# A streaming encoder layer (RWKV-7 and forgetting attention): modulation tiles in groups, and the steps of each stage given one by one

## The chip, the cores and the metric

The kernel runs on one core of a Trainium2 chip. The metric is the device time of one execution, in microseconds (us). The kernel before takes 1701.49 us, the median of 3 runs (1700.19 to 1702.09); the profiled execution took 1699.15 us.

## The reference, cut to what matters

One layer of width 1024 over 1024 prompt frames of one stream and 64 new frames of another (with 256 past frames in a cache). `c` is a conditioning vector for each stream; the six modulation vectors that come of it are what the change groups.

```
mod = silu(c) @ w_ada + b_ada                       # 1024 -> 6 x 1024, per stream
sh1, sc1, gt1, sh2, sc2, gt2 = split(mod, 6)
h = rms_norm(x, norm1_g) * (1 + sc1) + sh1
proj = h @ w_in                                     # RWKV: r, k, v, three small ones; FoX: q, k, v, f
z = p + (previous row of p - p) * shift_mu          # the RWKV columns
... decay, a, g from small two-layer products; kk = normalized k
y_rwkv = (groupnorm(scan of s = s*w + (s @ -kk)(kk*a) + v k) + bonus) * g      # 8 heads x 64
y_fox = softmax(q k / 8 + decay bias, causal) @ v                              # 8 heads x 64
x = x + gt1 * (concat(y_rwkv, y_fox) @ w_out)
h2 = rms_norm(x, norm2_g) * (1 + sc2) + sh2
x = x + gt2 * ((silu(h2 @ w_gate) * (h2 @ w_up)) @ w_down)
```

Outputs are x and the new states, keys, values and log forget values, all in fp32.

## The kernel before, in words

Activations lie with the 1024 columns on partitions (8 tiles of 128, index k) and the frames along the free axis. Half 0 is the prompt's frames 0 to 511, half 1 the frames 512 to 1023 with the 64 new frames behind them (576, in two pieces of 288). Large products keep fp32 accuracy by splitting both operands into a high and a low part: `mm3` (L289 to L296) issues three matmuls for each k, whi times xhi (L294), whi times xlo (L295), wlo times xhi (L296). `split` casts the high part on ScalarE (L212) and subtracts on VectorE (L216).

**Modulation.** `mod` has 48 column tiles of 128: 0 to 7 are sh1, 8 to 15 sc1, 16 to 23 gt1 and so on. For one tile, `ada_mm` (L182) issues 8 matmuls with 32 columns of `ct` as the stationary operand (columns 0 and 1 are silu(c) of the two streams, the others zero); four k at a time write four strips of 32 partitions. ScalarE copies the result into `mrow` (L193). `ada_fin` (L195) transposes it on TensorE (L198), sums the four strips on VectorE (`mred`, L200) and adds the bias (`mod`, L201). `gains` (L203, L204) makes (1 + sc) * norm_g.

**The stages.**
1. The start: x is loaded and its statistics are taken; the 16 tiles of sh1 and sc1 are computed in the order 0, 8, 1, 9, ...; whenever a pair is there, `h_part` makes that k's part of h: x times gain on VectorE (L270), `hhi` on ScalarE (L271), `hlo` on VectorE (L272). Two w_in tiles (12 and 13) are split beside it.
2. Phase of half 0, then of half 1: `phase` (L1295) walks the string ORDER[half], whose letters are steps for a pair of heads: Z the three RWKV projections, D, A, B, N the decay, the chunk matrices, the scan, the output norm, Q, K, V, q, k the FoX projections and norms. `proj` (L298) takes one modulation tile off a list (`background`, tiles 16 to 39) before each w_in tile that it loads in half 0.
3. Attention of half 0, then of half 1: `Pipe` keeps three units (a pair of query blocks of a head) in flight. After head 0's units of half 1, `residual_x` and `load_mix` bring in half 0's rows: `load_mix` (L980) reads 8 tiles of 128 x 512 from a scratch in HBM (L984) through a pool of two buffers ("fs") and splits each (`mixrh`, `mixrl` for RWKV, `mixfh`, `mixfl` for FoX). Then after every head comes one `outproj` tile of half 0 (`po`).
4. The output projection of half 1, the FFN (tiles 40 to 47 of the modulation, gt2, are computed at its start: 40 to 43 among half 0's first FFN products and 44 to 47 before half 1's), and the down projection.

A tile scheduler sets the order of the instructions on every engine. It works from the order in which the program issues them and from modelled finish times, so a step that is issued earlier is spread among what stands there. Each engine then executes its own list in order, and a transfer is issued from SP's list, in order as well.

Of the kernel before, what the change touches and what calls it, by code (L numbers as in the profile page):

```python
# [16 lines left out]
P = 128  # L17
# [17 lines left out]
ORDER = ("Z0 D0 A0 D1 Z1 L Q0 B0 V0 N0 A1 C0 Z2 D2 q0 O A2 K0 k0 B1 K1 V2 Z3 D3 Q1 q1 V1 C1 A3 S k1 Q2 N1 q2 Q3 B2 N2 K2 k2 V3 K3 k3 C2 q3 C3",  # L35
         "Z0 T3 L D0 A0 Z1 U3 D1 B0 Q0 A1 D2 K0 Z2 A2 k0 D3 Q1 q0 N0 B1 K1 k1 q1 Z3 A3 N1 V0 V1 B2 V2 Q2 N2 q2 K3 Q3 q3 P B3 K2 k3 k2 V3")
# [28 lines left out]
class K:  # L65
# [7 lines left out]
    def consts(self):  # L73
# [14 lines left out]
        self.ct = c.tile([P, KT, 32], F32, name="ct")  # L88
        nc.gpsimd.memset(self.ct, 0.0)
        nc.vector.tensor_tensor(self.ct[:, :, 0:2], cc.rearrange("p (b k) -> p k b", b=2),  # L90
# [90 lines left out]
    def ada_mm(self, t, raw=None, ptag="mm"):  # L181

        nc = self.nc
        if raw is None:
            raw = self.ada_load(t)
        ps = self.ps([P, 2, P], tag=ptag, name="pada")
        for s in range(2):
            for i in range(4):
                k = 2 * i + s
                last = nc.tensor.matmul(ps[32 * i:32 * i + 32, 0], self.ct[:, k], raw[:, k], start=(s == 0),  # L190
                                        stop=(s == 1))
        row = self.slot([P, P], name="mrow", tag="mrow")
        return t, ps, row, last, nc.scalar.copy(row, ps[:, 0])  # L193

    def ada_fin(self, part):  # L195
        nc = self.nc
        t, ps, row = part[:3]
        self.last = nc.tensor.transpose(ps[:, 1], row, self.ident)  # L198
        red = self.slot([P, 2], name="mred", tag="mred")
        nc.vector.tensor_reduce(red, ps[:, 1].rearrange("p (i b) -> p b i", i=4)[:, 0:2], axis=AX.X, op=ALU.add)  # L200
        nc.vector.tensor_scalar(self.mod[:, t], red, self.vc[:, V_BADA + t:V_BADA + t + 1], None, op0=ALU.add)  # L201
# [215 lines left out]
    def rwkv_a(self, hf, j, z, d):  # L417
# [29 lines left out]
        for h in range(2):  # L447
# [6 lines left out]
            bon[:, off:off + m], ps, zv[:, off:off + m], op=ALU.mult), "ra")  # L454

        At = self.rpool.tile([P, 9, 2, 2, 64], F32, tag="At", name="At")
        for c in range(0, nch, 4):
# [7 lines left out]
            for h in range(2):  # L465
                nc.vector.tensor_tensor(At[:, c:c + m, :, h], pa[h][:, 0:m].rearrange("p i (x t) -> p i x t", x=2),
                                        self.amask[:, h:h + 1].rearrange("p o (x t) -> p o x t", x=2)
                                        .to_broadcast([P, m, 2, 64]), op=ALU.mult)

# [30 lines left out]
    def rwkv_b(self, hf, j, st):  # L500
# [14 lines left out]

        def small(name, blocks, mm):
# [20 lines left out]
        for h in range(2):  # L537
            for x in range(2):
                r = 64 * h + 32 * x
                nc.scalar.copy(inv[r:r + 16, 0:nch, r + 16:r + 32], pg[h][r:r + 16, 0:nch, 16:32])  # L540

# [16 lines left out]
        nc.gpsimd.memset(rk[64:128, 0:nch, 0:64], 0.0)  # L558

# [9 lines left out]
        for t0 in range(0, nch, 8):  # L569
# [6 lines left out]
            for x in range(min(2, m)):  # L576
                for h in range(2):
                    nc.scalar.copy(sv[64 - 64 * h:128 - 64 * h, t0 + x:t0 + m:2, h],
                                   pt[64 * x:64 * x + 64, 0:(m - x + 1) // 2, 64 * h:64 * h + 64])

# [8 lines left out]
        for c in range(nch):  # L589
            if c == 8:  # L590
# [385 lines left out]


# [310 lines left out]
    def phase(self, hf, order, late):  # L1288
# [13 lines left out]
        d, z, st, y, y0, f = {}, {}, {}, {}, {}, {}  # L1302
        for t in order:
            op, j = t[0], int(t[1]) if len(t) > 1 else 0
            if op == "D":
                d[j] = self.rwkv_d(hf, j, zl)
            elif op == "Z":
                zk = self.proj_z(hf, 4 + j)
                sq = self.slot(name="sq", tag="sa")
                nc.scalar.activation(sq[:, 0:hf.n], zk[:, 0:hf.n], AF.Square, scale=self.vc[:, V_KK + j:V_KK + j + 1])  # L1310
                z[j] = zk, self.proj_z(hf, j), self.proj_z(hf, 8 + j), sq
            elif op == "A":
                st[j] = self.rwkv_a(hf, j, z.pop(j), d.pop(j))
            elif op == "B":
                y[j] = self.rwkv_b(hf, j, st.pop(j))
            elif op == "N":
                self.rwkv_n(hf, j, y.pop(j), zg)
            elif op == "T":
# [404 lines left out]
```

## Time and profile before

| | |
|---|---|
| median of 3 runs | 1701.49 us |
| profiled execution, its own time | 1699.15 us |
| its span, first to last instruction | 1697.5 us |
| mean granted TensorE clock | 0.992 |
| TensorE matmul busy | 1645.3 us, 97% |
| VectorE, ScalarE, GpSimd busy | 1124.8, 726.5, 183.1 us |

The kernel spends 0 to 36 us in the start, to about 334 in the phase of half 0, to about 737 in that of half 1 (the attention of half 0 lies over its end, from about 665 to 745), to about 905 in the attention of half 1 and half 0's output projection, to 953 in half 1's output projection; the FFN takes it to 1431 and the down projection to the end. A row of the timeline gives the start, the duration, the engine, the line of the code, the operation, output<-inputs and in brackets the idle time of the engine just before, with what ended it. A row of the windows gives busy time and number of instructions of each engine in that stretch, then the granted clock, the share of DMA time and GB/s.

### The profile page before, as it was taken

Reading aid. Unit: us, or ns where it says so; the run is one execution under the profiler, and the core shown is the slowest. Engines: PE = TensorE matmul, PEld = TensorE weight load, DVE = VectorE, ACT = ScalarE, POOL = GpSimd, SP = SyncE. Lnnn points to the kernel's source line nnn. Section 1 sums busy time; section 2 is a strip of 40 time slices with the busy share of each in tenths; the row PEclk is TensorE's granted clock in tenths of the full one; section 3 lists DMA queues with packets and bytes.
Section 4 is the critical chain, followed back from the end, with each engine's and each line's share of the span. In section 5 each row is a group of like instructions: output and inputs, shape, how many; then the busy total and the mean of one; then the engine's idle time right before and its main releaser. Section 6 shows DMA issues by size and latency. Waiting matters only on the chain.

```text
span 1697.5 us, 33265 instructions
## 1 busy us (share of the span) xinstructions
PE 1645.3 (97%) x12897; PEld 1439.1 (85%) x12897; DVE 1124.8 (66%) x2573; ACT 726.5 (43%) x1530; POOL 183.1 (11%) x412
## 2 busy tenths in 40 slices
PE   6999999999999999989999999999999999999999
PEld 3776776788888888767889899999999999999998
DVE  6776676757867655877877975555555556545545
ACT  4535364653545346766776633333333333211210
POOL 2102230222121213201120000000000000000000
PEclk9999999999999999989999999999999999999999
DMA  8544447541233344566654432222222215323313
GB/s 308 164 128 133 141 135 200 176 123 33 71 85 85 87 135 113 149 190 179 169 181 167 157 127 77 77 77 77 77 77 77 77 65 196 134 79 97 97 40 121
DMA packets 133580, 207.08 MB, mean 122 GB/s; under 512 B 62126, under 2 KB 70350, under 8 KB 133422
## 3 DMA queue, kind: packets, MB, share of 16 engines
q1 hardware_dynamic: 133422, 204.95, 39.5%
q8 instruction: 102, 1.67, 0.4%
q14 instruction: 56, 0.46, 0.1%
HBM read 157.65 MB, written 47.25 MB: 121 GB/s over the span
## 4 chain that ended last, share of the span: by engine, by line
PE 84%; DVE 6%; ACT 4%; DMA 3%; issue 2%; SPq 0%; POOL 0%; ACTq 0%; DVEq 0%; POOLq 0%
PE pd L1275 15%; PE pfe L1160 8%; PE pfc L1160 7%; PE pfa L1160 7%; PE pmm L294 5%; PE pmm L295 5%; PE pmm L296 5%; PE pfb L1160 4%; PE pbs L375 2%; PE pav L962 2%; PE po L294 2%; PE ppt L940 2%; PE po L296 2%; PE po L295 2%; PE pA L464 2%
## 5 line engine op out<-in xcount | busy, mean ns | idle before, releaser
L294 PE MATMUL pmm<-hhi,whi 128*128 128x288 f32 (+1 forms) x624 | 218.8, 351 | 2.3 <-ACT pb L317 1.4
L295 PE MATMUL pmm<-hlo,whi 128*128 128x288 f32 (+1 forms) x624 | 217.0, 348 | 0.0
L296 PE MATMUL pmm<-hhi,wlo 128*128 128x288 f32 (+1 forms) x624 | 215.2, 345 | 0.6 <-DVE wlo L216 0.6
L212 ACT CAST whi<-wraw 128x1024 fp32r<-128x1024 f32 (+2 forms) x116 | 99.2, 855 | 212.5 <-PE pd L1275 167.0
L1275 PE MATMUL pd<-ah,wlo 128*128 128x512 f32 (+1 forms) x528 | 173.5, 329 | 0.0
L1275 PE MATMUL pd<-al,whi 128*128 128x512 f32 (+1 forms) x528 | 173.3, 328 | 0.0
L1275 PE MATMUL pd<-ah,whi 128*128 128x512 f32 (+1 forms) x528 | 173.1, 328 | 0.0
L1279 DVE SCALAR_TENSOR_TENSOR x1t<-pd,mod,x1t 128x512 f32<-128x512 f32 x192 | 91.4, 498 | 111.5 <-PE pd L1275 111.0
L294 PEld LDWEIGHTS pmm<-hhi,whi 128*128 128x128 f32 x624 | 119.0, 191 | 14.1 <-ACT pb L317 2.0
L296 PEld LDWEIGHTS pmm<-hhi,wlo 128*128 128x128 f32 x624 | 118.7, 190 | 10.9 <-issue 1.7
L295 PEld LDWEIGHTS pmm<-hlo,whi 128*128 128x128 f32 x624 | 118.7, 190 | 9.9 <-issue 1.2
L216 DVE TENSOR_TENSOR wlo<-wraw,whi 128x1024 fp32r<-128x1024 f32 (+2 forms) x108 | 104.2, 965 | 18.8 <-ACT whi L212 18.3
L1275 PEld LDWEIGHTS pd<-al,whi 128*128 128x128 f32 x528 | 99.4, 188 | 7.7
L1275 PEld LDWEIGHTS pd<-ah,whi 128*128 128x128 f32 x528 | 99.3, 188 | 7.7
L1275 PEld LDWEIGHTS pd<-ah,wlo 128*128 128x128 f32 x528 | 99.3, 188 | 7.5
L1160 PE MATMUL pfc<-hh,hS 128*128 128x256 f32 (+1 forms) x352 | 101.6, 289 | 1.6 <-ACT hh L1062 1.6
L1160 PE MATMUL pfc<-hl,hS 128*128 128x256 f32 (+1 forms) x352 | 101.9, 289 | 0.0
L1160 PE MATMUL pfa<-hh,whi 128*128 128x256 f32 (+1 forms) x352 | 101.9, 290 | 0.0
L1160 PE MATMUL pfa<-hl,whi 128*128 128x256 f32 (+1 forms) x352 | 101.8, 289 | 0.0
L1160 PE MATMUL pfc<-hh,lS 128*128 128x256 f32 (+1 forms) x352 | 101.5, 288 | 0.0
L1160 PE MATMUL pfa<-hh,wlo 128*128 128x256 f32 (+1 forms) x352 | 101.4, 289 | 0.0
L604 POOL TENSOR_SCALAR sd<-sv,pc 64x64 f32<-64x64 f32 x136 | 76.3, 561 | 181.2 <-DVE sv L617 157.6
(361 smaller groups left out, 4383.5 us busy)
## 6 DMA issues: line engine op xcount, KB each, us to landing
wraw<-in_w_in_dram SPq DMA_DIRECT2D x52, 512.0 KB
wada<-in_w_ada_dram SPq DMA_DIRECT2D x48, 512.0 KB
as<-actscr SPq DMA_DIRECT2D x22, 544.0 KB
wraw<-in_w_gate_dram SPq DMA_DIRECT2D x22, 512.0 KB
wraw<-in_w_up_dram SPq DMA_DIRECT2D x22, 512.0 KB
wraw<-in_w_down_dram SPq DMA_DIRECT2D x40, 256.0 KB
wraw<-in_w_out_dram SPq DMA_DIRECT2D x16, 512.0 KB
actscr<-sg SPq DMA_DIRECT2D x22, 288.0 KB
```

The source lines that it names most:

```text
L212: nc.scalar.copy(hi, src)
L216: eng.tensor_tensor(lo, src, hi.bitcast(F32), op=ALU.subtract)
L294: nc.tensor.matmul(ps[0:M, 0:n], whi[:, k, 0:M], xhi[:, k, off:off + n], start=(k == 0), stop=False)
L295: nc.tensor.matmul(ps[0:M, 0:n], whi[:, k, 0:M], xlo[:, k, off:off + n], start=False, stop=False)
L296: nc.tensor.matmul(ps[0:M, 0:n], wlo[:, k, 0:M], xhi[:, k, off:off + n], start=False, stop=(k == kt - 1))
L375: nc.tensor.matmul(ps[:, 0:n], w, x[:, off:off + n], start=True, stop=True)
L464: nc.tensor.matmul(pa[h][:, i], kb[hp, c + i], rk[hp, c + i], start=True, stop=True)
L604: nc.gpsimd.tensor_scalar(sd[hsl[h]], sv[hsl[h], c, h], pc[hsl[h], c], None, op0=ALU.mult)
L940: nc.tensor.transpose(pt[0:rows, b - b0, t * P:t * P + qn], p[0:qn, pc:pc + rows], self.ident[0:qn, 0:qn])
L1160: nc.tensor.matmul(ps, l[:, k], r[:, s, k], start=(first and k == 0 and y == 0), stop=(k == 3 and y == 2), skip_group_check=True)
L1275: nc.tensor.matmul(ps[:, 0:n], w[:, i], x[:, t:t + n], start=(i == 0 and y == 0), stop=(i == len(fs) - 1 and y == 2))
L1279: nc.vector.scalar_tensor_tensor(dst, ps[:, so - off:so - off + l], self.mod[:, 40 + o, b:b + 1], dst, op0=ALU.mult, op1=ALU.add)
```

## The change

- `ct` has 38 columns with silu(c) at columns 6 and 7. `ada_mm` takes a list of tiles; tile number x of a group uses the columns 6 - 2x to 38 - 2x, so that its result lands in rows 2x and 2x + 1 of each strip, and all tiles of a group add into one PSUM tile. One copy, one transpose, one sum and one bias addition follow for the group. Groups are pairs (k, 8 + k) at the start, pairs (t, t + 1) in the background list (12 pairs), and 40 to 43 and 44 to 47 as fours. In the built program the 384 modulation matmuls stay; transposes, `mrow` copies, `mred` sums and `mod` additions go from 48 to 22 each.
- At the start `h_part` follows every pair, and both w_in splits are issued in the last two rounds (k = 6 and 7).
- Z is split into X (k projection and its square), Y (r), W (v); a G is one background pair. `rwkv_a` and `rwkv_b` yield between their parts, and "*n" in ORDER gives n steps. ORDER[1] says the same order as before but for a few steps.
- The order of the attention is written out as a table ATT of unit numbers; M (`load_mix` of half 0) stands before head 0's units of half 1 and R (`residual_x`) after three units; before, both stood behind all of head 0's units.

```diff
-ORDER = ("Z0 D0 A0 D1 Z1 L Q0 B0 V0 N0 A1 C0 Z2 D2 q0 O A2 K0 k0 B1 K1 V2 Z3 ...
+ORDER = ("W0 X0 G Y0 D0 A0*3 D1 X1 G Y1 W1 B0 L G Q0 B0*10 G B0 V0 N0 A1*3 C0 G Y2 X2 G W2 ...
+ATT = (...
+       "M H0 0 1 0 R 2 1 0 H1 3 2 1 4 3 2 5 4 3 O0 H2 6 5 4 7 6 5 8 6 7 O1 H3 ...
...
-    def ada_mm(self, t, raw=None, ptag="mm"):
+    def ada_mm(self, ts, raw=None, ptag="mm"):
...
+        for x, r in enumerate(raw):
+            for s in range(2):
+                for i in range(4):
+                    k = 2 * i + s
+                    last = nc.tensor.matmul(ps[32 * i:32 * i + 32, 0], self.ct[:, k, 6 - 2 * x:38 - 2 * x], r[:, k],
+                                            start=(x == s == 0), stop=(x == len(ts) - 1 and s == 1), skip_group_check=True)
...
     def ada_fin(self, part):
...
         self.last = nc.tensor.transpose(ps[:, 1], row, self.ident)
+        red = self.slot([P, 8], name="mred", tag="mred")
+        nc.vector.tensor_reduce(red[:, 0:2 * n], ps[:, 1].rearrange("p (i b) -> p b i", i=4)[:, 0:2 * n], axis=AX.X, op=ALU.add)
+        t = slice(ts[0], ts[-1] + 1, d)
+        u = slice(V_BADA + ts[0], V_BADA + ts[-1] + 1, d)
+        nc.vector.tensor_tensor(self.mod[:, t], red[:, 0:2 * n].rearrange("p (n b) -> p n b", b=2),
+                                self.vc[:, u].unsqueeze(2).to_broadcast([P, n, 2]), op=ALU.add)
...
     def proj(self, hf, col, evac):
...
-            if self.background:
-                self.background.pop(0)()
...
+    def att_phase(self, hf, order, more):
+        units = {}
+        for t in order:
+            if t[0] == "H":
+                us = self.attend(int(t[1:]), hf)
+                units.update({int(t[1:]) * len(us) + i: u for i, u in enumerate(us)})
+            elif t.isdigit():
+                next(units[int(t)], None)
+            else:
+                more[t[0]](int(t[1:] or 0))
...
+                pair = lambda k: self.ada_mm([k, 8 + k], raw[2 * k:2 * k + 2], "ch" if k % 2 else "ra")
+                nxt = pair(0)
+                for k in range(KT):
+                    part = nxt
+                    if k + 1 < KT:
+                        nxt = pair(k + 1)
+                    with tc.issue_after(nxt[3].ins):
+                        self.ada_fin(part)
+                    self.gains(self.g1[:, k:k + 1], 8 + k, V_N1 + k, 1)
+                    with tc.issue_after(nxt[4].ins):
+                        if k > 5:
+                            self.pre.append(self.split_w(w.pop(0), [P, KT, P]))
+                        self.h_part(hf, k, x0[:, k], rs)
+            self.background = [lambda t=t: self.ada_fin(self.ada_mm([t, t + 1])) for t in range(16, 40, 2)]
```

**First place: VectorE at the end of the start.** x is h's normalized part of one k (the last three k are seen), hlo its low part, wlo the low part of a w_in tile. Before:

```order
50 L204 SCALAR_TENSOR_TENSOR g_161<-mod,vc 128x2
51 L270 SCALAR_TENSOR_TENSOR x_189<-x_189,g_161,xacc 128x512
52 L200 TENSOR_REDUCE mred<-pada 128x2
53 L201 TENSOR_SCALAR mod<-mred,vc 128x2
54 L216 TENSOR_TENSOR wlo<-wraw,whi 128x1024
55 L272 SCALAR_TENSOR_TENSOR hlo<-x_189,mod,hhi 128x512
56 L200 TENSOR_REDUCE mred<-pada 128x2
57 L201 TENSOR_SCALAR mod<-mred,vc 128x2
58 L200 TENSOR_REDUCE mred<-pada 128x2
59 L204 SCALAR_TENSOR_TENSOR g_161<-mod,vc 128x2
60 L201 TENSOR_SCALAR mod<-mred,vc 128x2
61 L270 SCALAR_TENSOR_TENSOR x_189<-x_189,g_161,xacc 128x512
```

The change there (its line numbers are 15 to 18 higher):

```order
39 L288 SCALAR_TENSOR_TENSOR x_189<-x_189,g_161,xacc 128x512
40 L290 SCALAR_TENSOR_TENSOR hlo<-x_189,mod,hhi 128x512
41 L215 TENSOR_REDUCE mred<-pada 128x4
42 L218 TENSOR_TENSOR mod<-mred,vc 128x2x2
43 L215 TENSOR_REDUCE mred<-pada 128x4
44 L222 SCALAR_TENSOR_TENSOR g_161<-mod,vc 128x2
45 L218 TENSOR_TENSOR mod<-mred,vc 128x2x2
46 L288 SCALAR_TENSOR_TENSOR x_189<-x_189,g_161,xacc 128x512
47 L234 TENSOR_TENSOR wlo<-wraw,whi 128x1024
48 L222 SCALAR_TENSOR_TENSOR g_161<-mod,vc 128x2
49 L234 TENSOR_TENSOR wlo<-wraw,whi 128x1024
50 L290 SCALAR_TENSOR_TENSOR hlo<-x_189,mod,hhi 128x512
```

Rows 51 of before and 39 of the change are x of the same k (the sixth). The first `wlo` stood before that k's `hlo`; it now stands behind the next k's x, and the second `wlo` comes ahead of the last two `hlo`.

**Second place: ScalarE where the two attentions meet.** p is a block of probabilities, pth the high part of its transpose, avt the result of a unit. Before:

```order
789 L953 CAST pth<-ppt 128x128
790 L967 COPY avt<-pav 64x256
791 L922 ACTIVATE p,ls<-psc,nm 128x640
792 L922 ACTIVATE p,ls<-psc,nm 128x768
793 L926 ACTIVATE p<-p,ls 128x640
794 L922 ACTIVATE p,ls<-psc,nm 128x896
795 L953 CAST pth<-ppt 128x512 x2
796 L212 CAST mixrh_9540<-mixt 128x512 x2
797 L922 ACTIVATE p,ls<-psc,nm 128x1024
```

The change:

```order
760 L947 ACTIVATE p,ls<-psc,nm 128x128
761 L230 CAST mixrh_9400<-mixt 128x512
762 L978 CAST pth<-ppt 128x512
763 L978 CAST pth<-ppt 128x256
764 L992 COPY avt<-pav 64x256
765 L947 ACTIVATE p,ls<-psc,nm 128x256
766 L230 CAST mixrh_9400<-mixt 128x512
767 L978 CAST pth<-ppt 128x128
768 L951 ACTIVATE p<-p,ls 128x256
769 L947 ACTIVATE p,ls<-psc,nm 128x384
770 L978 CAST pth<-ppt 128x256
771 L992 COPY avt<-pav 64x256
```

Row 791 of before is half 1's first block; the casts of the mixed rows stood behind it, and now four of them stand among half 0's last units.

**Third place: SP's list of transfers there.** fy are half 0's attention rows, y the last RWKV rows of half 1, q2x, k2x, qsx, k1x, vsx the operands of half 1's heads. Before:

```order
428 L974 DMA yscr_71<-fy 128x512
429 L996 DMA x_0_9536<-in_x_dram 128x1024 x2
430 L984 DMA mixt<-yscr_71 128x512 x2
431 L868 DMA qsx_9562<-qx 128x576
432 L870 DMA k1x_9564<-kx 64x1344 x2
433 L984 DMA mixt<-yscr_71 128x512 x2
434 L873 DMA q2x_9563<-qx 64x576
```

The change:

```order
412 L1021 DMA mixt<-yscr_71 128x512 x2
413 L671 DMA yscr_72<-y 128x576
414 L898 DMA q2x_9418<-qx 64x576
415 L904 DMA vsx_7894<-vscr_110 128x512
416 L899 DMA k2x_9420<-kx 64x1344
417 L999 DMA yscr_71<-fy 128x512
418 L1021 DMA mixt<-yscr_71 128x512
419 L898 DMA q2x_9418<-qx 4x576
420 L899 DMA k2x_9420<-kx 4x1344
421 L1021 DMA mixt<-yscr_71 128x512
422 L901 DMA vsx_9421<-vscr_103 128x1280
```

The first two loads stood behind the last `fy` row and now stand two `fy` rows and one `y` row earlier; the next ones stand between the operands of half 1's first head.

## Rows read from the trace of the kernel before

**Rows 1.** The profile's page: the span, the busy time of each engine, and the chain of work that ended last, by engine.

```profile
span 1697.5 us, 33265 instructions
PE 1645.3 (97%) x12897; PEld 1439.1 (85%) x12897; DVE 1124.8 (66%) x2573; ACT 726.5 (43%) x1530; POOL 183.1 (11%) x412
...
PE 84%; DVE 6%; ACT 4%; DMA 3%; issue 2%; SPq 0%; POOL 0%; ACTq 0%; DVEq 0%; POOLq 0%
```

**Rows 2.** The windows of the span, by stage (busy us and instructions of each engine, granted clock, DMA share, GB/s).

```profile
50.00:334.00 284.00, 276.72 (x2251) 200.54 (x2249) 201.38 (x539) 139.95 (x289) 54.28 (x110) 0.99 0.53 153
...
738.00:742.00 4.00, 2.51 (x13) 1.68 (x13) 3.13 (x9) 2.32 (x7) 0.15 (x2) 0.92 0.67 253
742.00:754.00 12.00, 10.72 (x36) 8.24 (x37) 5.87 (x11) 4.70 (x10) 0.41 (x2) 0.50 0.74 217
754.00:766.00 12.00, 11.44 (x67) 8.61 (x66) 9.40 (x21) 9.08 (x21) 0.35 (x2) 0.96 0.51 151
766.00:772.00 6.00, 4.59 (x23) 3.40 (x23) 3.66 (x7) 3.22 (x7) 0.00 (x0) 1.00 0.46 144
...
800.00:950.00 150.00, 149.98 (x984) 131.48 (x983) 121.44 (x222) 100.14 (x195) 21.64 (x31) 1.00 0.54 165
950.00:984.00 34.00, 30.49 (x309) 26.19 (x308) 30.98 (x59) 25.26 (x48) 0.00 (x0) 1.00 0.43 146
```

**Rows 3.** The modulation's sums on VectorE and copies on ScalarE, all 48 of each: duration in ns (least, median, most), first and last start.

```profile
L200 DVE TENSOR_REDUCE mred<-pada x48: 147/159/168, 16.9 to 983.9; 128x2 f32<-128x8 f32 x48
...
L193 ACT COPY mrow<-pada x48: 245/265/273, 15.6 to 982.8; 128x128 f32<-128x128 f32 x48
```

**Rows 4.** The timeline of VectorE in the start.

```profile
18.80 0.75 DVE L270 SCALAR_TENSOR_TENSOR x<-x,g,xacc 128x512 f32<-128x512 f32 x1
...
20.34 0.75 DVE L272 SCALAR_TENSOR_TENSOR hlo<-x,mod,hhi 128x512 fp32r<-128x512 f32 x1 [0.45 <-ACT hhi L271]
21.01 0.16 DVE L200 TENSOR_REDUCE mred<-pada 128x2 f32<-128x8 f32 x1
21.21 0.31 DVE L201 TENSOR_SCALAR mod<-mred,vc 128x2 f32<-128x2 f32 x1
21.55 0.16 DVE L204 SCALAR_TENSOR_TENSOR g<-mod,vc 128x2 f32<-128x2 f32 x1
21.75 0.75 DVE L270 SCALAR_TENSOR_TENSOR x<-x,g,xacc 128x512 f32<-128x512 f32 x1
...
33.21 0.75 DVE L270 SCALAR_TENSOR_TENSOR x<-x,g,xacc 128x512 f32<-128x512 f32 x1
...
34.21 1.22 DVE L216 TENSOR_TENSOR wlo<-wraw,whi 128x1024 fp32r<-128x1024 f32 x1
35.35 0.75 DVE L272 SCALAR_TENSOR_TENSOR hlo<-x,mod,hhi 128x512 fp32r<-128x512 f32 x1
...
39.80 1.41 DVE L272 SCALAR_TENSOR_TENSOR hlo<-x,mod,hhi 128x512 fp32r<-128x512 f32 x2
```

**Rows 5.** The timeline of TensorE in the start and at the first projection.

```profile
14.50 1.93 PE L190 MATMUL pada<-wada,ct 128*32 128x128 f32 x30
...
17.77 0.33 PE L198 MATMUL pada<-ident,mrow 128*128 128x128 f32 x1
...
35.53 0.78 PE L294 MATMUL pmm<-hhi,whi 128*128 128x512 f32 x1
...
36.53 0.63 PE L296 MATMUL pmm<-hhi,wlo 128*128 128x512 f32 x1
36.96 0.63 PE L294 MATMUL pmm<-hhi,whi 128*128 128x512 f32 x1
...
38.24 0.41 PE L294 MATMUL pmm<-hhi,whi 128*128 128x512 f32 x1
```

**Rows 6.** The timeline of TensorE around two background tiles of the phase of half 0.

```profile
49.15 0.50 PE L294 MATMUL pmm<-hhi,whi 128*128 128x512 f32 x1 [0.36 <-ACT pb L317]
...
49.72 0.39 PE L296 MATMUL pmm<-hhi,wlo 128*128 128x512 f32 x1
49.95 0.40 PE L294 MATMUL pmm<-hhi,whi 128*128 128x512 f32 x1
50.19 0.27 PE L198 MATMUL pada<-ident,mrow 128*128 128x128 f32 x1
...
50.54 0.40 PE L296 MATMUL pmm<-hhi,wlo 128*128 128x512 f32 x1
...
77.76 0.50 PE L294 MATMUL pmm<-hhi,whi 128*128 128x512 f32 x1 [0.81 <-ACT pb L317]
```

**Rows 7.** The chain of work that ended last, between 755 and 775 us: start, us, what.

```profile
763.00 0.68 DVE mixrl L216
...
763.71 3.40 DMA mixt<-yscr
...
767.14 0.63 ACT mixfh L212
...
768.51 3.78 DMA mixt<-yscr
```

**Rows 8.** The timeline of TensorE at the start of half 1's FFN, the waits on `hh`, the high part of h2.

```profile
973.85 0.40 PE L1160 MATMUL pfc<-hh,hS 128*128 128x288 f32 x1 [1.57 <-ACT hh L1062]
974.90 0.41 PE L1160 MATMUL pfe<-hh,hS 128*128 128x288 f32 x1 [0.66 <-ACT hh L1062]
```

More of the change, by code (lines that the diff above doesn't have):

```diff
@@ L558, in rwkv_b @@
         nc.gpsimd.memset(rk[64:128, 0:nch, 0:64], 0.0)
+        yield
         kbt = kb
@@ L1338, in phase @@
[L1338 to L1341 removed]
+            for _ in range(int(times or 1)):
+                if op == "D":
+                    d[j] = self.rwkv_d(hf, j, zl)
+                elif op == "X":
+                    zk = self.proj_z(hf, 4 + j)
+                    sq = self.slot(name="sq", tag="sa")
+                    nc.scalar.activation(sq[:, 0:hf.n], zk[:, 0:hf.n], AF.Square, scale=self.vc[:, V_KK + j:V_KK + j + 1])
+                    z[j, 0], z[j, 3] = zk, sq
+                elif op == "Y":
+                    z[j, 1] = self.proj_z(hf, j)
+                elif op == "W":
+                    z[j, 2] = self.proj_z(hf, 8 + j)
+                elif op == "G":
+                    self.background.pop(0)()
+                elif op == "A":
+                    step(t, lambda: self.rwkv_a(hf, j, [z.pop((j, i)) for i in range(4)], d.pop(j)), st, j)
+                elif op == "B":
+                    step(t, lambda: self.rwkv_b(hf, j, st.pop(j)), y, j)
+                elif op == "N":
+                    self.rwkv_n(hf, j, y.pop(j), zg)
+                elif op == "T":
+                    step(t, late[j][0], y0, j)
+                elif op == "U":
+                    late.pop(j)[1](y0.pop(j))
+                elif op == "L":
+                    self.logf(hf)
+                elif op == "O":
+                    self.ones_rows()
+                elif op in "QK":
+                    f[t] = self.fox_qk(hf, j, int(op == "K"))
+                elif op in "qk":
+                    self.fox_norm(hf, j, int(op == "k"), f.pop(t.upper()))
+                elif op == "V":
+                    self.fox_v(hf, j)
+                elif op == "C":
+                    self.cache_kv(j)
+                elif op == "P":
+                    self.early()
+                elif op == "S":
+                    self.rs1 = self.x_stat1()
@@ L1460, in run @@
             self.att_pools(att, R)
-            pipe = Pipe(2)
-            for hd in range(8):
-                pipe.run(self.attend(hd, halves[0]))
-            pipe.flush()
+            self.att_phase(halves[0], ATT[0].split(), {})
             at0.close()
@@ L1547, in ada_run @@
             def ada_run(part):
-                old = None
-                for t, r in part:
-                    new = self.ada_mm(t, r, "b")
-                    if old:
-                        self.ada_fin(old)
-                    old = new
-                self.ada_fin(old)
+                ts, rs = zip(*part)
+                self.ada_fin(self.ada_mm(list(ts), list(rs), "b"))
             def gap():
@@ L1606, in run @@
             self.down(halves, pre, x1t, lambda g, f: self.act_load(f, apools[g % 2]))
-class Pipe:
-    def __init__(self, skew):
-        self.skew, self.live = skew, []
-    def run(self, units):
-        for u in units:
-            self.live.insert(0, u)
-            self.step(self.skew)
-    def step(self, keep):
-        self.live = [u for u in self.live if next(u, None) is not None]
-        while len(self.live) > keep:
-            u = self.live.pop()
-            for _ in u:
-                pass
-    def flush(self):
-        while self.live:
-            self.step(len(self.live))
 class Rows:
```

119 lines of the change are left out of this document (34 added, 85 removed), and 7 rows, old and new, of tables (ATT, ORDER).

## The prediction

> **What bounds the kernel now.** I read the page first: TensorE's matmuls are busy for 1645.3 of 1697.5 us, VectorE for 1124.8 and ScalarE for 726.5, and 84% of the chain that ended last is TensorE's [rows 1]. So only what TensorE does, and the 52.2 us in which it does nothing, can move the time. Then I read the windows by stage: they show where those 52.2 us are, and where the clock is low [rows 2]. The phase of half 0, 50 to 334 us, has 284.0 - 276.7 = 7.3 us idle. From 738 to 772, where half 0's attention ends and half 1's begins, 34.0 - 29.26 = 4.74 us are idle and 12 us run at a granted clock of 0.50, which is the level of 1.2 GHz. From 800 to 950 TensorE is idle for 0.02 of 150 us: the units that the new table permutes there hide nothing that could come out. From 950 to 984 it is idle for 3.5 us, with VectorE busy for 30.98 of 34. In the built program the order on TensorE and on SP from 334 to about 737 us is that of before but for one spot, and from 985 us to the end it is the same; I count nothing there. After that come the timelines of single places, one for each term below.
>
> **The start.** Two things change: two tiles of one k share a copy, a transpose, a sum and an addition, and the two weight splits stand elsewhere. The pace per k is VectorE's: x starts at 18.80, hlo at 20.34 after waiting for ScalarE's hhi, then sum, addition, gain and the next x at 21.75, so 1.54 + 0.67 + 0.20 + 0.34 + 0.20 = 2.95 us [rows 4]; from the first x to the sixth it is (33.21 - 18.80) / 5 = 2.88 [rows 4]. The sum and addition that go stood between x and hlo, in the wait for hhi, which ScalarE ends: removing 0.4 us there makes that wait longer and the pace no shorter. So 8 sums and 8 additions fewer are worth nothing here, and if the cover (the wait for hhi, 0.45) were gone they would be worth 8 x 0.4 = 3.2. The first x is a little later: TensorE now does 31 modulation matmuls ahead of the first transpose. 15 of them take 30 rows of the trace and 1.93 us from 14.50 [rows 5]; 31 end at about 18.1 with the second half of them at the higher clock, where the transpose that x waits for stood at 17.77 [rows 5]. That is 0.4 us, so the sixth x is at 33.6. Then the moved splits count. The first wlo ran at 34.21, ahead of the sixth hlo [rows 4]; now it stands behind the sixth hlo, two sums, two additions, a gain and the seventh x. From 33.6: 1.54 to hlo, 0.67 for it, five small ones at 0.2 and x with 0.67 give 37.5, and wlo (1.14 until the next can start, 34.21 to 35.35) ends at 38.7. TensorE starts the first projection at 35.53, and at 36.53 it uses wlo in its third matmul [rows 5]; in the new order it has four matmuls ahead of that, 0.43 each (36.53 to 36.96), some 35.9 + 1.7 = 37.6. It waits **1.1 us**. The matmuls run at half clock there until 38.24 [rows 5], 0.2 us dearer each; the wait keeps it there for perhaps four more, **0.8**. Together **+2**. The bounds: 0 if the clock returns meanwhile and wlo is on time, +4 if the last hlo, which two wlo now precede (it ended at 41.2; now 1.54 + 0.67 after an x at 40.7, 43), is waited for as well.
>
> **The phase of half 0.** Twelve transposes go. One costs TensorE little: matmuls stand 0.23 us apart (49.72 to 49.95), and from 49.95 to 50.54 there are two of them and a transpose in 0.59, so 0.12 for it [rows 6]; 12 x 0.12 = **-1.4**. The copies, sums and additions run on engines with room (VectorE 201, ScalarE 140 of 284 us [rows 2]; a sum takes 159 ns, a copy 265 [rows 3]), and go for nothing. A modulation tile takes one of the two PSUM buffers of the projections, so the next projection may wait for ScalarE's copy of the last one: 0.36 and 0.81 us [rows 6]. With half as many groups I take those two away: **-1.2**. Against it, the finer steps put pieces of the scan's chain next to each other with less between them; no row prices that, and I take **+1.2**, one more wait of the size of each of the two. Net **-1.4**. The bounds are -5 (two thirds of all 7.3 us idle) and +3 (as much again as those 1.2, plus 2 from the transposes' removal, since they filled holes).
>
> **Where the attentions meet.** Before, the eight loads of half 0's mixed rows go out behind the last rows of half 0, through two buffers; the chain that ended last runs through them: 3.40 us and 3.78 us of load with a split between [rows 7]. The output projection's matmuls (0.23 each) that need them therefore come after 755 us, although TensorE has holes from 738 on. Now the first two loads are issued three stores earlier, ScalarE's four first casts stand among half 0's last units, and twelve output matmuls stand ahead of half 1's first score block, six more behind its second. Twelve are 12 x 0.23 = 2.8 us of work; the holes from 738 to 754 are 1.49 + 1.28 = 2.8 [rows 2]. I take **-2.8**. From 766 to 772, where they waited for the loads, 1.41 us are idle [rows 2]: **-1.4**. What the early casts delay: four casts of 0.63 are 2.5 us of ScalarE, which is busy for 2.32 of 4 us from 738 to 742 [rows 2]; I let half of it fall on the path, **+1.2** (0 to 2.5). The clock: 10.72 us of work at 0.50 from 742 to 754, and shares at 0.92 and 0.96 beside it, cost 5.4 + 0.2 + 0.4 = 6.0 us against full clock [rows 2]. It fell after 4 us in which TensorE worked for 2.51 [rows 2]; those holes are only partly filled, since the twelve matmuls stand at their end, so I take a quarter, **-1.5**. Sum **-4.5**; bounds -10.2 (2.8 + 1.4 + 6.0) and +2.
>
> **The FFN's start.** Eight modulation tiles become two groups: six transposes fewer, 6 x 0.12 = **-0.7**. Sums and additions on VectorE fall by 12, which sets the pace here; TensorE's waits on the FFN's input are 1.57 and 0.66 [rows 8], and the 32 matmuls of the second group come in one piece ahead of half 1's products, where such a wait stands. I take 1.3 of those 2.2: **-1.3**. Sum **-2**; bounds -3.5 (all that is idle [rows 2]) and +1 (a group waits for the last of four weight tiles).
>
> **Sum.** 2 - 1.4 - 4.5 - 2 = -5.9. The profiled execution took 1699.15 and would take 1693.2; the median of the runs is 2.3 above it, so 1695.5.
>
> **Rivals.**
> *The early loads become a wait (slower).* ScalarE and SP work their lists in order. A cast that stands ahead of its load's arrival holds the pth and avt behind it, on which half 0's last units depend. The third and fourth casts reuse the two buffers, so each comes a load (3.40 to 3.78 [rows 7]) after a split; if nothing covers it, 2 x 3.6 = 7.2 us fall on the path and the gains of 5.7 there don't come: +2 - 1.4 + 7.2 - 2 = +5.8, **1707.3**. For it: TensorE did wait at those loads before. Against it: the list puts four and more instructions between two casts. It decides where these take less than a load.
> *The clock stays where it was and the start costs its bound (no change).* +4, -1.4, in the meeting -4.2 + 2.5, and -1 in the FFN: -0.1, **1701.4**. For it: nothing in the list fills the sparse stretch ahead of 738.
> *The clock never falls (a larger gain).* If the twelve matmuls keep TensorE busy enough, the other 4.5 us of the clock come too: **1691**, and 1689 if the start costs nothing.
> *A pair holds its PSUM buffer too long.* From 36 to 334 us the groups share two buffers with the projections, and a pair's second eight matmuls hold one 0.6 us longer. A buffer is wanted again after 24 matmuls of 0.23, 5.6 us, so it should be hidden; if not, 12 x 0.6 = 7 us come on top: **1702.5**. The Trainium skill (Perfetto Trace Analysis, section Matmuls under Optimizing Tensor Performance) speaks for this rival: independent matmul groups should rotate through PSUM banks so that emptying one overlaps the next one's matmuls. A longer group in one bank goes against that, and the two waits for pb agree with it [rows 6].
> *The change doesn't do what it says.* The built program has the 26 transposes fewer and the matmuls all there, so this is left with no chance of its own.
>
> **How the numbers follow.** My forecast gets 0.53, the early loads as a wait 0.11, no change 0.19, the larger gain 0.12, the PSUM buffer 0.05. A measurement of this kernel tells 0.2%, 3.4 us, from no change: faster is below 1698.1, slower above 1704.9. Of my forecast I count 0.05 as not below 1698.1. Faster 0.48 + 0.12 = 0.60; same 0.05 + 0.19 + 0.05 = 0.29; slower 0.11. The range reaches from 1687, two below the larger gain's lower figure, to 1703, past the PSUM rival; outside are the slower rival and a little below.
>
> **What would show it.** Right: the first projection starts with a wait for wlo of about 1 us; the granted clock still falls near 741 but the half-clock stretch is shorter than 12 us; output matmuls stand before 745; waits on mixt's casts near 771 are gone; 950 to 984 is 2 us shorter. Wrong: ScalarE idle on mixt between 730 and 745 with TensorE waiting on pth or avt behind it; waits of projections on pb that are more than before; a start that is more than 4 us longer, or shorter.

## The result, and the profile after

The changed kernel takes 1704.51 us, the median of 20 runs (1701.61 to 1722.91), and the kernel before, beside it, 1700.49 (20 runs, 1697.81 to 1702.31). The ratio is 1.0037, 95% interval [1.0022, 1.0051]: slower, by 4 us in the medians and 6 by the ratio, where 1695.5 was forecast. The interval leaves out 1, so the sign is clear of the noise, but the difference is small: 1704.51 lies just under the 1704.9 from which the prediction would have called it slower. The profiled execution took 1704.81 us. One execution of an experiment below (the change, output tiles a head earlier) took 3084.25 us and is left out of its ratio.

Below I use one measure of the traces all along, the **lag**: the time at which a matmul runs in one trace minus the time at which the same matmul runs in the first trace of before, taken where the order on TensorE is the same in both. For the change:

| time in the trace of before, us | lag, us | what lies between this and the row above |
|---|---|---|
| 47.8 (48th projection matmul) | +2.4 | start |
| 340 | +3.6 | phase of half 0 |
| 382, then 394 | +3.7, +6.6 | a low-clock stretch in the same order |
| 732 | +6.0 | phase of half 1 |
| 790 | +6.4 | where the attentions meet |
| 950 | +11.2 | half 1's attention, both output projections |
| 1006 | +8.0 | start of the FFN |
| 1416, then 1690 | +9.0, +5.9 | FFN, down projection |

The page of the change: span, busy time, chain by engine.

```profile
span 1703.1 us, 33102 instructions
...
PE 1645.5 (97%) x12871; PEld 1441.8 (85%) x12871; DVE 1117.4 (66%) x2521; ACT 721.3 (42%) x1504; POOL 186.2 (11%) x412
...
PE 83%; DVE 6%; ACT 5%; DMA 3%; issue 2%; SPq 0%; POOL 0%; DVEq 0%; ACTq 0%; POOLq 0%
```

Against [rows 1], TensorE's busy time is the same, and VectorE's and ScalarE's are 7.4 and 5.2 us lower: the sums and copies went, and nobody was waiting for them. The windows of the change, by stage:

```profile
50.00:334.00 284.00, 276.35 (x2223) 200.42 (x2221) 196.92 (x511) 137.88 (x280) 56.81 (x109) 0.98 0.51 152
738.00:742.00 4.00, 3.05 (x17) 2.15 (x17) 3.66 (x11) 3.48 (x13) 0.49 (x3) 1.00 0.79 226
742.00:754.00 12.00, 10.16 (x55) 7.67 (x56) 9.05 (x23) 7.46 (x20) 0.94 (x6) 1.00 0.61 206
754.00:766.00 12.00, 9.48 (x38) 6.51 (x38) 8.21 (x16) 6.94 (x13) 0.00 (x0) 0.86 0.92 260
766.00:772.00 6.00, 5.76 (x35) 4.32 (x34) 3.65 (x9) 4.51 (x11) 2.39 (x1) 1.00 1.01 219
800.00:840.00 40.00, 34.50 (x196) 27.40 (x195) 31.43 (x62) 26.88 (x59) 6.17 (x12) 0.91 0.50 129
...
800.00:950.00 150.00, 144.49 (x904) 123.38 (x903) 116.76 (x218) 101.70 (x201) 22.40 (x33) 0.98 0.55 166
950.00:984.00 34.00, 32.46 (x338) 30.16 (x336) 31.21 (x54) 23.59 (x42) 0.00 (x0) 1.00 0.48 164
```

Beside [rows 2] two stretches decide. From 742 to 754 the clock is full, as I had hoped in part, but from 738 to 772 as a whole TensorE is idle for 5.5 us, and before for 4.7. And from 800 to 950, where before TensorE was idle for 0.02 us, it is idle for 5.5 us, all of it between 800 and 840, and the clock falls there as well. The timeline of TensorE in the change shows the first output matmul (`po`) and the waits in this stretch:

```profile
744.23 0.50 PE L312 MATMUL po<-mixrh,whi 128*128 128x512 f32 x1
...
762.36 0.79 PE L312 MATMUL po<-mixfh,whi 128*128 128x512 f32 x1 [1.84 <-ACT mixfh L230]
...
804.37 0.50 PE L935 MATMUL psc<-k1x,qsx 128*128 128x512 f32 x1 [0.95 <-ACT p L947]
...
831.88 0.39 PE L987 MATMUL pav<-ptl,vsx 128*128 128x256 f32 x1 [1.87 <-DVE ptl L979]
...
838.23 0.50 PE L312 MATMUL po<-mixrh,whi 128*128 128x512 f32 x1
```

Before, the first and the 73rd output matmul:

```profile
755.94 0.40 PE L294 MATMUL po<-mixrh,whi 128*128 128x512 f32 x1
...
826.14 0.48 PE L294 MATMUL po<-mixrh,whi 128*128 128x512 f32 x1
```

The output matmuls start at 744.23, 11.7 us earlier than before. By the trace the 60th is done at 790.2 (before: 813.4), and the 73rd starts at 838.2 (before: 826.1). Between 803 and 838 none is there to run while a unit waits for its exponentials or its split. The 73rd needs the fourth tile of w_out. Its load stands in SP's list behind the `vsx` of head 4 (heads count from 0), which must wait for its buffer.

```profile
819.26 0.34 SPq L901 DMA_DIRECT2D vsx<-vscr  x1
...
820.21 0.58 SPq L300 DMA_DIRECT2D wraw<-in_w_out_dram  x1
```

Before, that load was issued at 811.74:

```profile
811.74 0.58 SPq L282 DMA_DIRECT2D wraw<-in_w_out_dram  x1
```

The 73rd itself does not wait in the trace: its weights were split by about 831, and it simply stands that late in TensorE's list. That the scheduler put it there because of the late load is argued here; two runs below test it.

The work done at the same point says what was moved. Where the attention has come as far as at 790 us in before, 66 output matmuls have run in the change and 43 before. These 23, 5.3 us at 0.23 each, were taken in with a lag that grew by only 0.4 us from 732 to 790. From there to 950 the change has 23 fewer to run, and its lag still grows by 4.8.

The wait at 762.36 is on the last mixed row, which the chain of waits follows back to half 0's last store, 4.06 us before its load could go out:

```profile
752.08 4.06 DMA yscr<-fy
```

### The profile page after: what moved, and what is told of

Same layout as the page of the kernel before. It is cut to its first block, busy times and chain, and to the rows that moved or that the text cites. A ratio compares the mean times of both kernels' runs of the same rounds, so it can differ in the third digit from the quotient of the medians.

```text
span 1703.1 us, 33102 instructions
## 1 busy us (share of the span) xinstructions
PE 1645.5 (97%) x12871; PEld 1441.8 (85%) x12871; DVE 1117.4 (66%) x2521; ACT 721.3 (42%) x1504; POOL 186.2 (11%) x412
## 4 chain that ended last, share of the span: by engine, by line
PE 83%; DVE 6%; ACT 5%; DMA 3%; issue 2%; SPq 0%; POOL 0%; DVEq 0%; ACTq 0%; POOLq 0%
PE pd L1312 15%; PE pfe L1197 8%; PE pfc L1197 8%; PE pfa L1197 8%; PE pmm L312 5%; PE pmm L314 5%; PE pmm L313 5%; PE pfb L1197 4%; PE pbs L391 2%; PE pav L987 2%; PE po L312 2%; PE ppt L965 2%; PE po L314 2%; PE pA L481 2%; PE po L313 2%
## 5 line engine op out<-in xcount | busy, mean ns | idle before, releaser
L312 PEld LDWEIGHTS pmm<-hhi,whi 128*128 128x128 f32 x624 | 119.6, 192 | 12.3 <-ACT whi L230 2.3
L313 PEld LDWEIGHTS pmm<-hlo,whi 128*128 128x128 f32 x624 | 119.5, 192 | 10.4 <-issue 1.0
```

Source lines behind the costliest of these rows:

```text
L312: nc.tensor.matmul(ps[0:M, 0:n], whi[:, k, 0:M], xhi[:, k, off:off + n], start=(k == 0), stop=False)
L313: nc.tensor.matmul(ps[0:M, 0:n], whi[:, k, 0:M], xlo[:, k, off:off + n], start=False, stop=False)
```

## The experiments

Medians and ratios to before, in the order in which they are told:

| run | us | ratio, 95% interval |
|---|---|---|
| both attention tables as before | 1699.28 | 0.9995 [0.9982, 1.0008] |
| loads back, units permuted | 1704.31 | 1.0022 [1.0009, 1.0036] |
| early loads, units as before | 1709.03 | 1.0056 [1.0041, 1.0072] |
| early loads, units as before, output tiles a head earlier | 1701.66 | 0.9999 [0.9989, 1.0009] |
| the change, output tiles a head earlier | 1701.69 | 1.0008 [0.9997, 1.0019] |
| half 0's last units permuted alone | 1703.12 | 1.0017 [1.0002, 1.0031] |
| start's splits back | 1703.16 | 1.0015 [0.9999, 1.0032] |
| FFN tiles single | 1706.44 | 1.0045 [1.0027, 1.0062] |
| all tiles single | 1733.43 | 1.0211 [1.0186, 1.0236] |
| before, FFN groups | 1726.45 | 1.0163 [1.0136, 1.0189] |
| before, background pairs and FFN groups | 1704.97 | 1.0028 [1.0016, 1.0041] |
| attention as before, start's splits back | 1697.75 | 0.9990 [0.9974, 1.0006] |

**The attention tables.** First, both tables back to before's order of units, loads and output tiles:

```diff
-"M H0 0 1 0 R 2 1 0 H1 ... H2 6 5 4 7 6 5 8 6 7 O1 ... O5 H7 21 21 20 19 22 21 20 23 O7 22 O6 22 23 23"
+"H0 0 1 0 2 1 0 R M H1 ... H2 6 5 4 7 6 5 8 7 6 O1 ... O5 H7 21 20 19 22 21 20 23 22 21 O6 23 22 23 O7"
```

> The change with both attention tables set back to the order of before (residual and mix loads behind head 0's units of half 1). Theory A (the early output matmuls are only borrowed: what they fill at 738 to 755 us is missed at 803 to 838): the time stays within 1.5 us of the change's, 1703 to 1706; the half-clock stretch of some 13 us near 745 is back and the 5.5 us of idle TensorE between 800 and 950 are gone. Rival B (the attention table is the loss, by its early loads): the time falls by 4 to 6 us, to 1699 to 1700.5.

It gave 1699.28, 5.2 below the change: rival B. My first theory was right in kind and wrong in its sum: borrowed matmuls cost more than they give. Its trace, 800 to 840:

```profile
800.00:840.00 40.00, 40.00 (x253) 33.19 (x252) 31.90 (x66) 29.06 (x65) 8.62 (x14) 1.00 0.56 151
```

No idle time. The half-clock stretch near 745, which theory A wanted back, did not come, although the order is before's there; with it gone, the lag fell from +1.3 at 732 us to -1.1 at 790. The run on the layout of buffers, below, is without it too and falls by 2.5. So the whole low stretch of [rows 2] was worth some 2.4 us, not the 6.0 that I had worked out: at full clock TensorE is idle longer in the same order, for 6.8 and 6.7 us from 738 to 772 in these two runs against 4.7.

One trace is a thin base for a lag, so here are all with an order in common. From 732 to 950 the lag grew by 5.2, 2.8 and 4.7 us in the three traces with the change's order there (the change, start's splits back, FFN tiles single), and moved by -2.3 to +0.9 in the five others with before's order. The scatter lies ahead of 790, with the clock; from 790 to 950 it is 4.8 to 5.0 against 0.0 to 0.9. With the start's splits back the change's order met no low stretch from 732 to 790, and its lag fell by 2.2 there, before's order without one by 2.4 and 2.5: the early output matmuls were taken in at next to no cost, and the loss comes behind them.

Then the two parts alone, the loads back (`R M` behind head 0's units, other units as in the change) and the early loads alone (units as before):

> The change with only the loads of half 0's mixed rows (and the residual) back behind head 0's units of half 1; the permuted units stay. Theory F (three output tiles have their weights ahead, 72 matmuls; with the early loads they are used up by 803 us and the fourth tile's weights come with the heads, so TensorE idles until 838): the loads are the loss, 1698.5 to 1700.5, no idle TensorE between 800 and 838. Rival H (the permuted units are the loss): 1703 to 1706 with the 5 us of idle time still between 800 and 838.

> The change with its early loads (and its place of the residual), but every unit of both attentions in before's order. In the built order 72 output matmuls are used up by the 180th pav matmul and none follow for 60 more, as in the change. Theory K (early loads and permuted units each cost, since either leaves TensorE without output matmuls or without ready blocks somewhere): between the two, 1701 to 1703.5, with idle time between 800 and 840 us. Rival L (the permuted units alone are the loss, as moving the loads back alone gave nothing): 1698.5 to 1700.5. Rival M (the loads are the whole loss): 1703.5 to 1705.5.

1704.31 and 1709.03. The first hit rival H's time, though its idle time between 800 and 838 was 1.2 us and not 5; the second missed all three ranges on the slow side. Against 1699.28 with neither, permuted units alone cost 5.0 us, early loads alone 9.7, and both together 5.2 (by the ratios to before 4.6, 10.4 and 7.1): they are not a sum; the permutation takes back a third to a half of what the early loads cost, and costs when alone. The window with the early loads alone:

```profile
800.00:840.00 40.00, 34.41 (x183) 27.05 (x182) 29.06 (x59) 25.10 (x56) 5.27 (x10) 0.83 0.50 138
```

Next, whether the missing output matmuls are the mechanism: every output tile is issued one head earlier, so that w_out's fourth tile is loaded earlier.

```diff
-"M H0 0 1 0 R 2 1 0 H1 ... O0 H2 ... O1 H3 ..."
+"M H0 0 1 0 R 2 1 0 O0 H1 ... O1 H2 ... O2 H3 ..."
```

> The change with its early loads, and every output tile of half 0 issued one head earlier, so that in the built order 24 more output matmuls stand between 800 and 840 us. Theory F: the idle time there goes, the lag against before at 850 us falls by 4 to 5, and the time comes to 1698.5 to 1701.5, unless the tiles are missed at the end of half 1's attention. Rival G (head 1's operands, queued behind SP's waits on the early loads, make half 1 late): 1703 to 1706.

> The change with early loads, units in before's order, and every output tile of half 0 issued one head earlier: beside the one with early loads alone (1709.0) it differs in the output tiles only; 24 more output matmuls stand before the 240th pav matmul. Theory F (the loss of the early loads is that output matmuls run out from 803 to 838 us): most of the 9.7 us comes back, 1699 to 1703, and TensorE's idle time between 800 and 840, 5.6 us there, falls below 2. Rival G (half 1's operands queue behind SP's waits on the loads): 1706 to 1709, the idle time stays.

From the change it took 2.8 us (1701.69), from the early loads alone 7.4 (1701.66). The window of the second:

```profile
800.00:840.00 40.00, 37.20 (x219) 29.83 (x218) 30.52 (x64) 28.27 (x63) 7.57 (x11) 0.96 0.59 154
```

Idle time fell from 5.6 to 2.8 us (I had said below 2), and the lag from 732 to 950 us grew by 3.1 in place of 9.8. That is theory F: only the place of the output tiles is changed, and the early loads are issued early in both. What is left, 2.4 us over the run with neither, stays open. Rival G is bounded by it: in the change the DMA share of the windows from 754 to 772 is 0.92 and 1.01 (before 0.51 and 0.46), and the load of head 1's `k1x` took 11.71 us, but TensorE waited only 0.24 us for it:

```profile
759.44 11.71 DMA k1x<-kx
```

```profile
771.19 0.50 PE L935 MATMUL psc<-k1x,qsx 128*128 128x512 f32 x1 [0.24 <-DMA k1x<-kx]
```

For the permutation, half 0's last units alone (`14 13 12 15 14 13 15 14 15` to `13 12 14 14 13 14 15 15 15`):

> The change with half 1's attention as before and only half 0's last units permuted. Theory P (the permutation's 5 us come from these last units, where TensorE has the fewest filling matmuls): 1702.5 to 1705. Rival Q (they come from half 1's permuted units): 1698 to 1700.5.

1703.12, in theory P's range, but the profile caught a 20 us low-clock stretch at 198 us, which has nothing to do with the edit; in it the lag from 732 to 950 grew by 1.7, against -2.3 to +0.9 with before's units and +3.8 with all permuted. From 790 to 950 alone it grew by 4.9, no less than with all permuted (4.5), though half 1's units are before's there. So these units can carry all of the permutation's loss; with one trace of each, and medians whose intervals overlap, how much is not settled.

**The start.** The two splits go back to the rounds in which they were:

```diff
-                        if k > 5:
+                        if k in (5, 7):
```

> The change with the two w_in splits of the start back in rounds k = 5 and 7. Theory A (the late wlo and the longer half-clock stretch cost the 2.35 us by which the 48th projection matmul is late): that matmul comes at 47.9 to 48.6 us, as before, and the time falls by 2 us, to 1702 to 1703. Rival C (the first 36 us are paced by VectorE and the pairs, wherever the splits stand): the 48th matmul stays at 50.4 and the time at 1704 to 1705.

1703.16 is just above theory A's range, but the trace is plain. VectorE and TensorE in the change:

```profile
33.16 0.75 DVE L288 SCALAR_TENSOR_TENSOR x<-x,g,xacc 128x512 f32<-128x512 f32 x1
34.71 0.75 DVE L290 SCALAR_TENSOR_TENSOR hlo<-x,mod,hhi 128x512 fp32r<-128x512 f32 x1 [0.79 <-ACT hhi L289]
...
36.35 0.75 DVE L288 SCALAR_TENSOR_TENSOR x<-x,g,xacc 128x512 f32<-128x512 f32 x1 [0.33 <-DVE mod L218]
37.02 1.22 DVE L234 TENSOR_TENSOR wlo<-wraw,whi 128x1024 fp32r<-128x1024 f32 x1
```

```profile
35.82 0.79 PE L312 MATMUL pmm<-hhi,whi 128*128 128x512 f32 x1 [0.47 <-ACT whi L230]
...
38.29 0.80 PE L314 MATMUL pmm<-hhi,wlo 128*128 128x512 f32 x1 [0.30 <-DVE wlo L234]
...
42.23 0.39 PE L314 MATMUL pmm<-hhi,wlo 128*128 128x512 f32 x1
...
50.18 0.40 PE L314 MATMUL pmm<-hhi,wlo 128*128 128x512 f32 x1
```

With the splits back, TensorE:

```profile
34.59 0.78 PE L312 MATMUL pmm<-hhi,whi 128*128 128x512 f32 x1
...
37.18 0.39 PE L312 MATMUL pmm<-hhi,whi 128*128 128x512 f32 x1
...
46.78 0.40 PE L314 MATMUL pmm<-hhi,wlo 128*128 128x512 f32 x1
```

From the first to the 48th matmul the change takes 14.4 us, this 12.2, and before 12.3 and 12.1 in its two traces. The time of the first moves by 1 us between executions of one program, so the term is the difference, 2.1 us: 0.3 of waiting and the rest mostly half clock, until 42.2 instead of 37.2. The other traces bear it out: 13.9 to 15.2 us in seven more with the change's start, 12.4 in the other with the splits back, 12.1 in two more with before's start. In the medians it is 1.4 us, and there the two intervals overlap.

**The groups.** At the FFN's start, tiles one by one again:

> The change with the eight modulation tiles of the FFN's start taken one by one again. Theory A (the two groups of four are worth the 3.1 us by which the lag falls between 950 and 1006 us): the lag at 1006 us stays at that of 950 and the time rises by 3 us, to 1707 to 1708. Rival D (that stretch is shorter because its inputs come with more slack, not by the groups): within 1 us of the change's, 1703.5 to 1705.5.

1706.44, 1.9 more than the change, between the ranges of A and D. The lag moves by -0.2 from 950 to 1006 us, against -3.2 in the change; over all traces it moves by -0.8 to -3.2 in the eleven with the groups of four, median -1.8, and by -0.2 to +1.3 in the five others with single tiles. So the groups are worth some 2 us there, theory A at two thirds of its size, and -3.2 is the largest of eleven. Then all tiles single in the change's order, and groups put into the kernel before:

> The change's orders with every modulation tile taken alone (start, background, FFN), so the moves without the groups. Theory A (moves cost or give nothing, groups give 3 at the FFN and some 1 to 2 in the phase of half 0, the start's loss is that of the splits): 1705 to 1709. Rival E (the groups themselves cost, by holding a PSUM buffer longer and by making the first x later): 1699 to 1702.

> The kernel before with the groups of four at the FFN's start alone; every other tile is taken alone and the order is before's. Theory A (the two groups are worth 2 to 3 us, and the shorter down projection 2.5 more): 1696 to 1698.5. Rival (only one of the two comes): 1698.5 to 1700.5.

> As the one with groups at the FFN's start, and the background tiles in pairs ahead of every second projection; the start is before's, with single tiles. If the pairs are worth what their 12 transposes cost, 1.4 us: 1694.5 to 1697.5. Rival (a pair holds its PSUM buffer longer and pays the 1.4 back, or the scheduler's new order falls into low-clock stretches as the moves without groups did): 1697.5 to 1703.

All three missed their ranges, by 24, 26 and 2 us, and all three have another order on TensorE in both phases. Another way to issue the tiles gave the scheduler other modelled times, most likely; that is argued, not tested. The second groups tiles at the FFN alone and otherwise changes only the form of one small addition and the widths of `ct` and `mred`, yet its lag is +13.5 at 340 and +30.0 at 732 us; the third is at -4.3 at 340, the best of all, and at +5.1 at 732. So these three don't price a group; they show that the order of the phases is worth tens of us. The first, with two single tiles where the change has a pair, may lose most of it to the clock (0.967 on the mean, against 0.988, at most 37 of the 39 us between the profiled executions), so no cost of a tile can be read from it.

**Before once more, and where buffers lie.**

> The kernel before once more, for a second profile of the same program. Theory I (where the granted clock falls between 600 and 760 us changes from execution to execution, and the drift of +0.9 us in the FFN and -3.0 in the down projection that every variant shows against the first profile belongs to that one execution): the low stretches lie elsewhere, and the second profile drifts against the first by about the same -2 from 1006 us to the end. Rival J (clock and drift belong to the program): the stretch of 13 us at 741 is there again and no drift.

> The kernel before with one mred buffer in place of two in the FFN's pools, which moves what is allocated behind it by a few bytes per partition. Theory N (the down projection took 262.37 us from its first to its last matmul in both profiles of before and 259.84 to 259.89 in all eight of the variants because of where buffers lie, not of the order): 259.8 to 259.9 here. Rival O (something else that the variants share, such as the larger ct): 262.4.

> The kernel before with ct of 38 columns, of which its matmuls use the first 32, and one mred buffer in the FFN's pools; the order is that of the run on the layout. Theory R (where buffers lie decides the down projection's pace, and ct's 192 bytes per partition move them): from first to last matmul it takes 259.8 to 259.9 us, as in the variants. Rival S (something else): 261.7 to 262.4.

The second profile of before (1699.84) had low stretches at 746 and 767 in place of 741, and no drift: theory I for the clock, rival J for the drift. The down projection takes 262.37 us in both, 259.84 to 259.89 in every variant. One `mred` buffer less gave 261.7, neither theory; with the wider `ct` besides, in the same order on every engine, it took 259.85: theory R. The page's group of the matmuls that take `wlo`, the third of each three, for before's second profile and for the wider `ct`:

```profile
L1275 PE MATMUL pd<-ah,wlo 128*128 128x512 f32 (+1 forms) x528 | 173.4, 328 | 0.0
```

```profile
L1275 PE MATMUL pd<-ah,wlo 128*128 128x512 f32 (+1 forms) x528 | 172.2, 326 | 0.0
```

**The best version.** Attention tables as before and the splits back, with all groups:

> The change with both attention tables of before and the two splits of the start back in rounds 5 and 7. If the two losses add (5.2 of the first experiment, 1.4 to 3.4 of the second): 1695.5 to 1698, faster than both. Rival (what the start gives is lost again to the clock or to waits in the phase of half 0): 1698.5 to 1700.5.

1697.75, inside the range that I gave for the sum, 6.8 below the change; against before the interval [0.9974, 1.0006] takes in no difference, so it beats the change and is not shown to beat both.

## Why the prediction was wrong, point by point

- **The start**: +2 forecast, +2.1 measured, by the mechanism told: wlo behind the seventh x (37.02), a wait for it (0.30 at 38.29; I had 1.1), and half clock for longer (I had 0.8, it is most of the term). The size is right partly by luck, since the two parts missed in opposite ways, and the sixth x came no later than before (33.16; I had 33.6).
- **The phase of half 0**: -1.4 forecast. From the 48th matmul to 340 us the lag moved by +1.2 in the change's profile, which has two low-clock stretches there, and by -0.3, -0.6, +0.2, -1.8, -0.5 and +2.1 in six others with the same order (+11.4 in a seventh, with the 20 us stretch told of above). The median of the six is -0.4. Before's own program moved by +0.4, +1.4 and +3.7 in its three other traces, so the first trace is its best, and a gain of the size forecast is neither shown nor excluded: the scatter, in which the clock falls at other places, is larger than the term. Waits of projections on pb, 0.36 and 0.81 before [rows 6], are gone from TensorE's waits, and 7 us more did not come: the rival of the PSUM buffer fell. The Trainium skill (Perfetto Trace Analysis, section Matmuls under Optimizing Tensor Performance), which spoke for it, states that independent groups should rotate through PSUM banks. In the trace no projection waits on pb with pairs in one bank. With single tiles in the change's order none does either (one modulation tile waits 0.8 us), so the order of the phase may have done it, and not the smaller number of groups.
- **Where the attentions meet**: -4.5 forecast, +5.2 measured. This is the step that failed, at "the units that the new table permutes there hide nothing that could come out". TensorE was busy without a hole from 800 to 950 because output matmuls filled the holes of half 1's units. The early ones, 23 by the same point of the attention, were taken from there, and the fourth output tile did not follow: its weights are loaded with head 4. I priced the holes filled as a gain, -2.8 and -1.4, and not the holes laid open: 5.5 us, and two low-clock stretches of 3.4 us in them. The filling itself worked, 5.3 us of matmuls for 0.4 us of lag, but it gives nothing unless the stretch that the matmuls are taken from gets shorter, and that one grew by 4.8 us. The permuted units cost by themselves too (5.0 us in the medians, alone); I had put them at nothing, and how they cost stays open. The early loads did not hold up TensorE for long (my slower rival: waits of 0.25 and 1.84 us for a mixed row, not 7.2), so the slower time came by a mechanism that I had not named.
- **The clock**: the 6.0 us of [rows 2] were an upper bound that I cut to a quarter, 1.5; its whole worth was some 2.4. The low stretch there comes and goes with the same order: 13.7 us in one trace of before's program, 10.2 and 6.8 in two others, none in the fourth.
- **The FFN's start**: -2 forecast, -3.2 on this trace, -1.8 in the median of eleven and 1.9 in the medians of the runs: right in size. Not by the wait that I named: the wait for hh fell only from 1.57 [rows 8] to 1.1, and all of TensorE's idle time between the same two matmuls from 3.5 to 2.3 us. Which work makes up the rest is not shown.

```profile
PE pfc L1197 <- ACT hh L1099: 1.1, 1, 1.1
```

- **Left out**: the down projection, 2.5 us shorter by where buffers lie, and +1.3 to 2.9 for a low-clock stretch at 385 us. That one came in the change and in eight of nine variants with its order there, and in two of the four profiles in which before's program runs up to that point; it goes with no step of the change that I can name, and its cause stays open.

By the lag: 2.4 + 1.2 + 2.9 - 0.5 + 5.2 - 3.2 + 0.9 - 3.0, with the last two for FFN and down projection, is +5.9, and the profiled executions differ by 5.7.

## What to carry to other kernels

A stage in which the bounding engine has no hole may be full because of filling work from elsewhere. Whoever moves that work forward should count how much of it is ready (here three weight tiles, 72 matmuls), where the next comes from, and what the stage looks like when it has run out; work that fills a hole is spent once. And a program whose order comes from a scheduler should be compared by its built order before a small edit is priced: two small edits moved the phases by some 30 us.

## What the runs showed of the hardware that I had not expected

The down projection runs 1% slower or faster with the same instructions in the same order, by where buffers lie: 262.37 us in both profiles of before, 261.7 with one small buffer fewer, 259.85 with 24 bytes per k tile more in `ct` besides. Which buffer and which address matter was not tried.

The granted clock fell near 387 us in the change while the profile shows TensorE at work almost without a hole, in an order that kept 1.00 in two of the four profiles of before's program:

```profile
380.00:384.00 4.00, 3.93 (x26) 3.23 (x25) 3.07 (x13) 3.41 (x10) 0.00 (x0) 1.00 0.23 90
384.00:388.00 4.00, 4.00 (x33) 4.00 (x32) 2.50 (x11) 2.95 (x7) 0.00 (x0) 0.86 0.04 5
388.00:392.00 4.00, 4.00 (x19) 4.00 (x19) 1.02 (x5) 1.79 (x3) 0.49 (x2) 0.50 0.00 0
```

Among the matmuls in these rows are many of 8 columns:

```profile
386.41 0.37 PE L735 MATMUL plc<-lacc,ones 128*128 128x8 f32 x2
```

The Trainium skill (TensorE: Matmul & The Clock Gate, section HAM oscillation — how this bites in real kernels) tells of falls behind waits, with cold work after them. At the start the change's trace agrees: the clock falls at 28.5 us, behind waits for w_ada tiles of up to 1.09 us. Near 387 us the trace shows a fall without such a wait; why it came there no run tells.
